# Where the steps of differential attention stand among the projections of a two-layer diffusion trunk

## The chip, the cores and the metric

The kernel runs on one core of a Trainium2 chip. A core has a matrix engine (TensorE, PE in the profile; its weight loads are PEld), a vector engine (VectorE, DVE), an activation engine (ScalarE, ACT), a general engine (GpSimd, POOL), and a queue from which all of this kernel's transfers are issued (SyncE, SP). The engines run side by side and wait for each other by semaphores; within one engine the order of instructions is fixed when the program is built. The metric is the device time of one execution in microseconds. Lower is better. The time before is the median of three runs.

## What is computed

Two layers run over 128 context tokens and 512 latent tokens, 640 columns in all. A layer projects its modulated input into nine parts, runs three mixers on them (a gated convolution, differential attention with 4 heads, latent attention with 8), projects their joined outputs back, and then runs a gated feed-forward block. The part that the change moves is the score and softmax of differential attention for the latent tokens:

```python
def diff_block(qb):
    sc = jnp.einsum("bhmqd,bhmkd->bhmqk", qb, k_all).astype(jnp.float32) * DIFF_SCALE
    p = jax.nn.softmax(sc, axis=-1)
    a = p[:, :, 0] - lam * p[:, :, 1]
    return jnp.einsum("bhqk,bhkd->bhqd", a.astype(v_all.dtype), v_all)
```

Each head has two maps of 32 features; the second, times a learned `lam`, is taken off the first. The keys are the 512 latent tokens and 128 cached ones. The latent attention that follows is an ordinary softmax over heads of 96 features, whose queries and keys are projected up from compressed rows (`cq`, `ckv`).

## The kernel before

Activations lie transposed, 128 features by 640 tokens. Token columns are split into region A (384 columns) and region B (256). A weight is split into a high and a low part, and so is an activation, so that one product is three matmuls (`matmul3`, line 338 on, with its matmul at L343). One `job` (L346) takes one 128-column block of a weight over both regions: with 8 blocks of features it is 24 matmuls for A and 24 for B.

The input projections run in the order `ax0 ac0 ab0 ax1 dk0 dq0 dk1 dq1 dv ckv0 ckv1 ac1 ab1 cq0 cq1 cq2` (`stage_in`, L1036). `dk` and `dq` are the keys and queries of differential attention, two head pairs each. After `dq0` and `dq1` the split rows are written to memory (`ddq`, `ddk`) and read back as 96-row tiles `dqp`, `dkp` that stack the three products (`assemble_diff`, L933; all through the sync queue, L273). `dv` (`dv_job`, L978, matmuls at L992) goes by token tiles, in the order 2, 0, 1, 3, 4, with 24 matmuls each. Then `attention` (L1449) runs up-projections: `k0` to `k3` (keys), `v0` to `v5` (values), `e0`, `e1` (rotary part of the queries) and `q0` to `q3` (queries), in the order of `JOBS` (L77). `q_job` (L1152) evacuates its result on ScalarE (L1160), splits it and writes it to memory (`qd`). `load_pair` (L1172) reads the queries and keys of two latent heads back as `mq` and `mk` (8 loads, and one more of `pd` for the context tokens).

Among these jobs, the kernel places attention work in numbered steps. `plan_steps` (L1380) makes a list: 32 differential steps (0 to 31: four units of 8 scores), then 32 latent ones. A differential step (`score` in `diff_unit`, L1215) is one score of 128 queries against 640 keys: two matmuls (L1192) into the PSUM buffer `sc`, the row maximum on VectorE (L1196), the exponential on ScalarE (L1207), the reciprocal (L1224), and the scaling on GpSimd (L1226) or, for the second map, the combination on VectorE (L1230). Other work is tied to step numbers: the products with the values (five parts for each unit; transposes at L1267, matmuls at L1278) lie four steps and more after their unit, `ASM` (L79) says after which steps the second head pair of `dqp` and `dkp` is assembled, and `LOADS` (L62) after which steps a latent pair is loaded.

`STEPS` (L72) and `JSTEPS` (L78) say how many steps each job runs. A pair is (in the middle, between regions A and B; at the end). The entries of `dv` count steps after each token tile, by the tile's number. From `dq1` on PSUM has two buffers for jobs and the single buffer `sc` for scores (`mm`, L239).

```python
ps = self.job(lambda k, p: u[:, p, 128 * k:128 * k + 128], h, NK, "AB", mid)
self.in_evac(l, n, ps, "AB")
...
self.step(end)
```

These places are the order in which the program is written down. When it is built, a planner sets each engine's queue: it follows the written order as a priority, with its own model of when each instruction would be ready, so that an instruction that it thinks not ready yet can be passed by later ones. The queue that comes out is fixed.

Of the kernel before, what the change touches and what calls it, by code (L numbers as in the profile page):

```python
# [58 lines left out]
ADV = 0  # L59
ACV = 2  # L60
HOLD = 2
LOADS = (29, 37, 43, 52)  # L62
SIDE = ((34, 37), (37, 40, 43), (36, 40), (47, 50, 56), (44, 47), (49, 51), (51, 54), (60, 62))
ADA_N = 12
ADA_IN = 1
# [3 lines left out]
ADA_FF2 = 1  # L69
ADA_LAG = 3  # L70
LAG = 4
STEPS = {"dv": (1, 2, 1, 1, 1), "ckv0": (0, 1), "ckv1": (0, 2), "ac1": (0, 2), "ab1": (0, 2), "cq0": (0, 2), "cq1": (0, 1), "dk1": (0, 0), "dq1": (0, 0)}  # L72
PAT = "PPPt"
PATC = "Pc"
CKS = 30
NP = 6
JOBS = "k0 k1 k2 k3 v0 v1 v2 v3 v4 e0 v5 e1 q0 q1 q2 q3".split()  # L77
JSTEPS = ((0, 1), (0, 1), (0, 1), (3, 0), (0, 1), (1, 0), (0, 0), (0, 0), (0, 1), (0, 2), (0, 0), (0, 0), (0, 1), (0, 0), (2, 1), (1, 0))  # L78
ASM = (9, 15)  # L79


WIN = (("ax0", 0), ("ac0", 512), ("ab0", 256), ("ax1", 128), ("dk0", 1024), ("dq0", 768), ("dk1", 1152),
# [110 lines left out]
class Trunk:  # L193
# [784 lines left out]
    def dv_job(self, l):  # L978
# [8 lines left out]
        for j in (2, 0, 1, 3, 4):  # L987
# [18 lines left out]
            self.tick()  # L1006
            self.step(STEPS["dv"][j])

# [27 lines left out]
    def stage_in(self, l):  # L1036
# [41 lines left out]
        for n in names[nskew:]:  # L1078
# [4 lines left out]
            else:  # L1083
                u = self.W.get((n, l))
                mid, end = STEPS.get(n, (0, 0))
                ps = self.job(lambda k, p: u[:, p, 128 * k:128 * k + 128], h, NK, "AB", mid)
# [293 lines left out]
    def plan_steps(self, l):  # L1380
# [7 lines left out]
        def put(step, *fs):  # L1388
            self.after.setdefault(step, []).extend(fs)
# [11 lines left out]
        def unit(kind, p, hf, n):  # L1401
            hold = {}
            g0 = len(self.steps)

            def start():
                hold["u"] = kind(l, p, hf)

            def step(i):
                if i == 0:
                    start()  # L1410
                hold["u"][0][i]()

            def av(kt):
                if kt == 0:
                    _, tiles, v, dst = hold["u"]
                    hold["av"] = self.av_steps(tiles, v, dst, hf)
                hold["av"][kt]()
            for i in range(n):
                self.steps.append(lambda i=i: step(i))
            for kt in range(5):  # L1420
                put(g0 + n - 1 + LAG + (n * kt) // 5, lambda kt=kt: av(kt))

        for kind, p, hf in units:
            unit(kind, p, hf, 8 if kind == self.diff_unit else 4)
        for g, i in enumerate(ASM):
            put(i, lambda g=g: self.assemble_diff(1, 2 * g, 2 * g + 2))
        for p, i in enumerate(LOADS):
            put(i, lambda p=p: self.load_pair(p))
# [20 lines left out]
    def attention(self, l):  # L1449
# [7 lines left out]
        kinds = {"k": self.k_job, "v": self.v_job, "e": self.qpe_job, "q": self.q_job}  # L1457
        for (kind, j), n in zip(JOBS, JSTEPS):
            n = n if isinstance(n, tuple) else (0, n)
# [251 lines left out]
```

## Time and profile before

| | before |
|---|---|
| median of 3 runs | 1777.19 us (1774.91 to 1778.72) |
| profiled execution | 1775.88 us |
| its span | 1774.1 us |
| TensorE busy | 1702.8 us |
| VectorE busy | 1021.1 us |
| ScalarE busy | 590.6 us |
| GpSimd busy | 420.0 us |

Times in the views are microseconds from the start of the span, of one profiled execution. In a timeline a line gives start, length, engine, line of code, operation, output and inputs, shape and count; in brackets stands how long the engine was idle before it and what released it. A group of matmuls of one kind is merged into one line. Matmuls overlap, so the last of a group ends somewhat into the next.

### The profile page before, as it was taken

What the parts mean: (1) busy time and instruction counts of PE and PEld (TensorE: products, weight loads), DVE (VectorE), ACT (ScalarE), POOL (GpSimd) and SP (SyncE); (2) the same over time, 40 slices, a digit from 0 to 9 for tenths busy, and PEclk for the clock granted to TensorE, in tenths of its full rate; (3) what the DMA queues carried; (4) which work ended last, traced back from release to release, by engine and by line L of the source; (5) the groups of instructions that cost most, each with busy time, mean ns of one, the idle gap of its engine ahead of it and who ended that gap; (6) DMA issues with size and microseconds to landing.
All of it is one profiled execution on the core that took longest, in us unless ns stands there. A gap on an engine that the chain in (4) does not pass through costs nothing. (4 is left out here: it accounts for less than half of the span.)

```text
span 1774.1 us, 29684 instructions
## 1 busy us (share of the span) xinstructions
PE 1702.8 (96%) x11983; PEld 1593.7 (90%) x11983; DVE 1021.1 (58%) x1824; ACT 590.6 (33%) x1010; POOL 420.0 (24%) x400
## 2 busy tenths in 40 slices
PE   8999989998999999999999899899989999999997
PEld 6998867698999999999989798677989999999997
DVE  3656776759566566856397558764682332232236
ACT  1334545525321121122243436554442212211221
POOL 0011113447701010110377111233582000000014
PEclk9999989999999999999989899899999999999998
DMA  9564584321355444544314544722122222222211
GB/s 333 196 204 140 168 250 145 109 90 48 101 149 150 149 136 140 174 130 150 93 51 166 170 113 149 210 64 84 48 75 81 72 75 81 64 79 84 68 53 59
DMA packets 100872, 217.38 MB, mean 123 GB/s; under 512 B 12160, under 2 KB 28928, under 8 KB 100736
## 3 DMA queue, kind: packets, MB, share of 16 engines
q1 hardware_dynamic: 100736, 215.50, 39.3%
q8 instruction: 94, 1.54, 0.4%
q14 instruction: 42, 0.34, 0.1%
HBM read 185.28 MB, written 30.18 MB: 121 GB/s over the span
## 5 line engine op out<-in xcount | busy, mean ns | idle before, releaser
L343 PE MATMUL mm<-h,wu 128*128 128x384 f32 (+1 forms) x4944 | 735.9, 310 | 0.2
L343 PEld LDWEIGHTS mm<-h,wu 128*128 128x128 f32 x4944 | 724.9, 189 | 6.9 <-issue 5.3
L142 ACT CAST wu<-stg 128x1024 fp32r<-128x1024 f32 (+2 forms) x200 | 201.5, 1011 | 701.3 <-issue 347.1
L144 DVE TENSOR_TENSOR wu<-stg,wu 128x1024 fp32r<-128x1024 f32 (+2 forms) x200 | 246.0, 1234 | 145.6 <-ACT wu L142 143.9
L343 PE MATMUL mm<-gh,wu 128*128 128x256 f32 (+1 forms) x1184 | 258.8, 310 | 0.0
L343 PEld LDWEIGHTS mm<-gh,wu 128*128 128x128 f32 x1184 | 198.7, 188 | 0.9 <-issue 0.6
L343 PE MATMUL mm<-gl,wu 128*128 128x384 f32 (+1 forms) x592 | 182.8, 309 | 0.0
L1196 DVE TENSOR_REDUCE nm<-mm 128x1 f32<-128x640 f32 x128 | 104.7, 818 | 54.7 <-PE mm L1192 53.8
L1545 DVE TENSOR_TENSOR gs<-gs,mm 128x640 f32<-128x640 f32 (+2 forms) x48 | 36.6, 763 | 152.7 <-PE mm L343 147.6
L653 DVE SCALAR_TENSOR_TENSOR x<-mm,ga,x 128x512 f32<-128x512 f32 x48 | 35.9, 749 | 146.2 <-PE mm L343 146.2
L672 POOL TENSOR_TENSOR accS<-x 128x640 f32<-128x640 f32 x4 | 10.0, 2490 | 443.6 <-DVE x L659 418.5
L343 PEld LDWEIGHTS mm<-gl,wu 128*128 128x128 f32 x592 | 111.4, 188 | 0.2 <-issue 0.2
L512 DVE SCALAR_TENSOR_TENSOR acc<-rawt,scT,acc 128x512 f32<-128x512 f32 x98 | 75.8, 773 | 57.8 <-DMA rawt<-in_w_ada 56.1
L364 PE MATMUL mm<-h,wu 128*128 128x384 f32 (+1 forms) x576 | 95.6, 329 | 1.0 <-DVE v L694 0.5
L364 PEld LDWEIGHTS mm<-h,wu 128*128 128x128 f32 x576 | 91.5, 206 | 3.3 <-issue 0.8
L343 PE MATMUL mm<-hi,wu 128*128 128x384 f32 (+1 forms) x400 | 89.8, 311 | 0.1
L510 POOL TENSOR_SCALAR acc<-rawt,scT 128x512 f32<-128x512 f32 x14 | 9.8, 701 | 313.0 <-PE tr L527 312.9
L1192 PE MATMUL mm<-mk,mq 96*128 96x384 f32 (+1 forms) x384 | 75.3, 337 | 5.8 <-ACT P L1207 2.3
L517 DVE SCALAR_TENSOR_TENSOR rawt<-rawt,scT 128x512 f32<-128x512 f32 x98 | 74.7, 763 | 2.1 <-POOL rawt L510 2.1
L1192 PEld LDWEIGHTS mm<-mk,mq 96*128 96x128 f32 x384 | 64.1, 201 | 12.7 <-ACT P L1207 4.9
L343 PEld LDWEIGHTS mm<-hi,wu 128*128 128x128 f32 x400 | 68.0, 188 | 2.6 <-issue 1.5
L1207 ACT ACTIVATE P<-mm,nm 128x640 f32<-128x640 f32 x56 | 44.6, 797 | 57.3 <-DVE nm L1196 45.0
(279 smaller groups left out, 2446.8 us busy)
## 6 DMA issues: line engine op xcount, KB each, us to landing
stg<-in_w_ff SPq DMA_DIRECT2D x104, 512.0 KB, 3.6
rawt<-in_w_ada SPq DMA_DIRECT2D x160, 256.0 KB, 3.0
stg<-in_w_in SPq DMA_DIRECT2D x30, 512.0 KB, 4.4
stg<-in_w_ff SPq DMA_DIRECT2D x32, 448.0 KB, 3.3
raw<-in_w_ada SPq DMA_DIRECT2D x32, 256.0 KB, 6.2
stg<-in_w_out SPq DMA_DIRECT2D x16, 512.0 KB, 4.3
mk<-kd SPq DMA_DIRECT2D x32, 240.0 KB, 5.8
mq<-qd SPq DMA_DIRECT2D x32, 192.0 KB, 5.5
```

Of the source, the lines that this page charges most:

```text
L142: nc.scalar.copy(u[:, 0, :ncol], t[:, :ncol])
L144: (nc.gpsimd if self.lo_pool else nc.vector).tensor_sub(u[:, 1, :ncol], t[:, :ncol], u[:, 0, :ncol].bitcast(F32))
L343: self.last = nc.tensor.matmul(out, w(k, pw), x(k, px), start=(k == 0 and i == 0), stop=(k == nk - 1 and i == 2)).ins
L364: self.last = nc.tensor.matmul(ps[:, c0:c1], u[:, pw, 128 * k:128 * k + 128], x(k, px)[:, c0:c1], start=(k == 0 and i == 0), stop=(k == nk ...
L512: nc.vector.scalar_tensor_tensor(self.acc[0], w, c[0], self.acc[0], ALU.mult, ALU.add)
L517: nc.vector.scalar_tensor_tensor(self.acc[1], w, c[1], self.acc[1], ALU.mult, ALU.add)
L653: nc.vector.scalar_tensor_tensor(lat(x), lat(ps), ga[:, 0, s, m:m + 1], lat(x), ALU.mult, ALU.add)
L672: nc.gpsimd.tensor_add(self.accS[:, c0:c1], self.first[0][:, c0:c1], x[:, c0:c1])
L1192: nc.tensor.matmul(ps[:, 128 + c0:128 + c1], q[:96, qc:qc + 128], k[:96, c0:c1], start=(i == 0), stop=(i == len(pairs) - 1))
L1196: nc.vector.tensor_reduce(nm, s, axis=AX.X, op=ALU.max, negate=True)
L1207: self.exp_end = nc.scalar.activation(P, s, AF.Exp, bias=nm, accum_out=sm).ins
L1545: nc.vector.tensor_mul(gs[:, c0:c1], gs[:, c0:c1], ps[:, c0:c1])
```

## The change

Constants only. The steps stand at other jobs; `ASM` and `LOADS` move by some steps.

```diff
-LOADS = (29, 37, 43, 52)
+LOADS = (28, 36, 43, 52)
...
-STEPS = {"dv": (1, 2, 1, 1, 1), "ckv0": (0, 1), "ckv1": (0, 2), "ac1": (0, 2), "ab1": (0, 2), "cq0": (0, 2), "cq1": (0, 1), "dk1": (0, 0), "dq1": (0, 0)}
+STEPS = {"dv": (1, 1, 0, 1, 1), "ckv0": (1, 1), "ckv1": (1, 1), "ac1": (1, 1), "ab1": (1, 1), "cq0": (1, 1),
+         "cq1": (1, 1), "cq2": (1, 1)}
...
-JSTEPS = ((0, 1), (0, 1), (0, 1), (3, 0), (0, 1), (1, 0), (0, 0), (0, 0), (0, 1), (0, 2), (0, 0), (0, 0), (0, 1), (0, 0), (2, 1), (1, 0))
-ASM = (9, 15)
+JSTEPS = ((0, 1), (0, 1), (0, 1), (0, 1), (0, 0), (0, 1), (0, 0), (0, 1), (0, 0), (0, 1), (0, 0), (0, 1), (1, 1), (1, 1),
+          (1, 1), (0, 0))
+ASM = (8, 12)
```

Counted out, so many of the 32 differential steps are written down by the end of each job:

| job | before | after |
|---|---|---|
| `dv`, after tiles 2, 0, 1, 3, 4 | 1, 2, 4, 5, 6 | 0, 1, 2, 3, 4 |
| `ckv0`, `ckv1`, `ac1`, `ab1` | 7, 9, 11, 13 | 6, 8, 10, 12 |
| `cq0`, `cq1`, `cq2` | 15, 16, 16 | 14, 16, 18 |
| `k0`, `k1`, `k2`, `k3` | 17, 18, 19, 22 | 19, 20, 21, 22 |
| `v0`, `v1`, `v2`, `v3`, `v4` | 23, 24, 24, 24, 25 | 22, 23, 23, 24, 24 |
| `e0`, `v5`, `e1` | 27, 27, 27 | 25, 25, 26 |
| `q0`, `q1`, `q2`, `q3` | 28, 28, 31, 32 | 28, 30, 32, 32 |

Before, most jobs of the input projections run two steps at their end; after, one in the middle and one at the end. The parts of the products with the values keep their step numbers and move with them. The second half of the `dqp`, `dkp` tiles is asked for after steps 8 and 12 instead of 9 and 15, the first latent pair after step 28 (middle of `q1`) instead of 29 (middle of `q2`), the second after 36 instead of 37. Both layers use the same constants. Instructions are neither added nor taken away.

## Rows read from the trace of the kernel before

**Rows 1.** The page: busy tenths and granted clock of TensorE, 40 slices

```profile
PE 1702.8 (96%) x11983; PEld 1593.7 (90%) x11983; DVE 1021.1 (58%) x1824; ACT 590.6 (33%) x1010; POOL 420.0 (24%) x400
PEclk9999989999999999999989899899999999999998
```

**Rows 2.** Windows, first layer: length, then busy by engine (instructions), clock, DMA share, GB/s

```profile
100.00:185.00 85.00, 83.33 (x630) 77.81 (x629) 51.55 (x107) 36.04 (x70) 13.55 (x15) 1.00 0.52 158
185.00:240.00 55.00, 53.27 (x366) 43.61 (x364) 44.53 (x90) 35.11 (x67) 7.10 (x7) 1.00 0.57 183
```

**Rows 3.** Timeline of TensorE, second layer, before and at the first score

```profile
959.82 11.91 PE L343 MATMUL mm<-h,wu 128*128 128x384 f32 x83
971.56 3.35 PE L992 MATMUL mm<-wu,h 128*128 128x288 f32 x24
982.19 0.87 PE L1192 MATMUL mm<-dkp,dqp 96*128 96x384 f32 x2 [7.28 <-DMA dkp<-ddk]
```

**Rows 4.** Timeline of the sync queue: first load of dkp, second layer

```profile
978.43 0.59 SPq L273 DMA_DIRECT2D dkp<-ddk  x1
```

**Rows 5.** Windows at low clock: length, TensorE busy (matmuls), clock, DMA share, GB/s

```profile
978.10:985.30 7.20, 3.11 (x13) 0.54 0.85 245
1016.30:1019.70 3.40, 3.40 (x13) 0.50 0.76 173
244.90:258.50 13.60, 11.04 (x47) 0.50 1.04 306
1118.80:1129.00 10.20, 7.63 (x26) 0.50 1.01 326
```

**Rows 6.** Timeline of TensorE, first layer: the first score

```profile
103.19 0.46 PE L1192 MATMUL mm<-dkp,dqp 96*128 96x384 f32 x2
```

**Rows 7.** Timeline of TensorE, first layer: last dv tile, fourth score

```profile
114.68 3.46 PE L992 MATMUL mm<-wu,h 128*128 128x288 f32 x24
...
119.55 0.45 PE L1192 MATMUL mm<-dkp,dqp 96*128 96x384 f32 x2
```

**Rows 8.** Timeline of TensorE: scores that waited, first and second layer

```profile
136.41 0.56 PE L1192 MATMUL mm<-dkp,dqp 96*128 96x384 f32 x2 [1.57 <-ACT Pt L1207]
...
1015.36 0.55 PE L1192 MATMUL mm<-dkp,dqp 96*128 96x384 f32 x2 [1.53 <-ACT Pt L1207]
```

**Rows 9.** Timeline of ScalarE, second layer, around the same place

```profile
1011.41 0.80 ACT L1207 ACTIVATE Pt<-mm,nm 128x640 f32<-128x640 f32 x1 [4.22 <-DVE nm L1196]
...
1012.19 0.68 ACT L892 COPY raw<-mm 128x640 f32<-128x640 f32 x1
```

**Rows 10.** Timeline of TensorE: last differential and first latent scores, both layers

```profile
243.05 0.56 PE L1192 MATMUL mm<-dkp,dqp 96*128 96x384 f32 x2 [1.89 <-ACT P L1207]
246.08 0.90 PE L1192 MATMUL mm<-dkp,dqp 96*128 96x384 f32 x2 [2.47 <-ACT P L1207]
...
249.29 1.65 PE L1192 MATMUL mm<-mk,mq 96*128 96x384 f32 x5 [0.40 <-DMA mk<-kd]
...
1117.54 0.56 PE L1192 MATMUL mm<-dkp,dqp 96*128 96x384 f32 x2 [1.89 <-ACT P L1207]
1119.94 0.90 PE L1192 MATMUL mm<-dkp,dqp 96*128 96x384 f32 x2 [1.83 <-ACT P L1207]
...
1124.77 1.65 PE L1192 MATMUL mm<-mk,mq 96*128 96x384 f32 x5 [1.23 <-DMA mk<-kd]
```

**Rows 11.** Timeline of TensorE, first layer: transposes of the probabilities

```profile
198.92 0.66 PE L1267 MATMUL tr<-first,Pt 128*128 128x128 f32 x4 [0.68 <-ACT PT L267]
```

**Rows 12.** Timeline of ScalarE, first layer: an exponential and the evacuation of q0

```profile
230.34 0.80 ACT L1207 ACTIVATE P<-mm,nm 128x640 f32<-128x640 f32 x1
...
231.12 0.70 ACT L1160 ACTIVATE mqs<-mm 128x640 f32<-128x640 f32 x1
```

**Rows 13.** Timeline of the sync queue, first layer: write of q0, first load

```profile
233.76 0.52 SPq L273 DMA_DIRECT2D qd<-lo  x1
...
237.39 0.54 SPq L273 DMA_DIRECT2D mq<-qd  x1
```

## The prediction

> **What bounds the kernel.** I read the page first. TensorE is busy for 1702.8 of 1774.1 us, so 71 us of its queue are idle, and the row of granted clocks falls below full speed in only a few of its forty slices [rows 1]. Anything worth having is therefore in the stretches where TensorE stands still or runs at 1.2 GHz. The windows by stage show where the change works: in the first layer the projections of the inputs (100 to 185 us) and the up-projections (185 to 240), in the second layer the same from 971 on. In the first layer TensorE is the fullest engine there, but VectorE is busy 51.55 of 85 us (61%) in the first stretch and 44.53 of 55 (81%) in the second, so a step that moves from the second to the first moves from a crowded place to a roomier one [rows 2]. Then I read TensorE's own queue in order of time, for every idle stretch and its releaser; the stretches that differential scores cause are the terms below. The profiled execution took 1775.88 us (span 1774.1), 1.3 under the median of the three runs, 1777.19. I make the sum against 1775.88 and move it by 1.3 at the end.
>
> **Part 1: the first score, one dv tile later.** In the second layer TensorE ends the first tile of `dv` (24 matmuls, 3.35 us) at 974.9 and then stands for 7.28 us before the first score, released by the load of `dkp` [rows 3]. That load is issued at 978.43 [rows 4]; its data come from `dq0`, through memory and back, so nothing of this path depends on how many dv matmuls have run. After the change one more tile of 24 matmuls stands ahead of the score. Its weights are those of the first tile, which has just run with them, so I take its time as the first one's, 3.35 us, and the wait left is 7.28 - 3.35 = 3.9 us. The clock: in 978.1 to 985.3 it averaged 0.54 with 3.11 us of work in it [rows 5]; work at half speed takes double, so this costs 3.11/2 = 1.6 us. The wait of 3.9 is longer than the 1.53 us that lowered the clock elsewhere (part 2), so I count no gain there. Value 3.35. Ends: 0, if the second tile can't start for want of a PSUM buffer until the score does; 7.28 + 1.6 = 8.9, if the planner sets the score later still. The value lies where the named work lies. In the first layer the same score started without a wait at 103.19 [rows 6], so moving it is worth nothing there; its cover is that TensorE has dv tiles to run instead.
>
> **Part 2: one score per half job instead of two at a job's end.** Before, six scores are due within `dv`, and then two at the end of each of four jobs. They can't keep that pace: in the first layer the last dv tile starts at 114.68, and the fourth score comes only at 119.55, in the next job [rows 7]. So scores queue up and meet. TensorE then waits 1.57 us at 136.41 and 1.53 us at 1015.36 for the exponential of the score ahead (only one PSUM buffer, `sc`, is for scores) [rows 8]. In the second layer the reason is to be seen in ScalarE's queue: it waits 4.22 us for a score's maximum, and the copy of `ckv0` that would free the other PSUM buffer stands behind that, at 1012.19 [rows 9]. There the clock fell too: 1016.3 to 1019.7 at 0.50 with 3.40 us of work, a cost of 1.7 us [rows 5]. After the change, 4 scores are due by the end of dv, then one per half job. Half a job is 24 matmuls; 83 take 11.91 us [rows 3], so 24 take 3.4 us. Successive scores that wait only for each other start 3.03 us apart in the first layer (243.05, 246.08) and 2.40 in the second [rows 10]. 3.4 is more than either, so a score's buffer is free when the next is due, and the pairs don't form. Value 1.57 + 1.53 + 1.7 = 4.8 us. Ends: 4.8, and below nothing: the planner times the whole list anew, and waits of the same kind (1.5 each, with a clock stretch 3.2) can form elsewhere: -3.2.
>
> On the clock, the row shows 1.53 us of idle time followed by half speed [rows 5, 8]. The Trainium skill ("TensorE: Matmul & The Clock Gate", Part 1: The HAM clock gate) says that the default is the low clock and that it returns after a whole idle window; by its figures such a short gap would not have lowered it, and the sum would lack the 1.7 us. The trace disagrees with that here, and the measurement decides.
>
> **Part 3: products with the values.** The five parts of each unit follow step numbers, which stay; two of them sat in `k3` with three scores and now lie one to a job. The wait of 0.68 us at 198.92, for the copy between transposes [rows 11], should go. Value 0.7, ends 0 and 0.7.
>
> **Part 4: the end of the differential scores.** Before, 16 steps are left from `k0` on, after 14: two scores leave the stretch where VectorE is at 81%. In before the last scores run with nothing beside them: 1.89 and 2.47 us of waits in the first layer, 1.89 and 1.83 in the second [rows 10], and the clock is at 0.50 in 244.9 to 258.5 with 11.04 us of work and in 1118.8 to 1129 with 7.63 [rows 5], costing 5.5 and 3.8. It looks as if 8.1 + 9.3 us could be had. But the loads for the first latent-attention heads end there as well: right after the last differential score TensorE waits for `mk`, 0.40 at 249.29 and 1.23 at 1124.77 [rows 10]. Their chain starts at `q0`: ScalarE evacuates it at 231.12 [rows 12], the write of its second half is issued at 233.76, the first load that reads it at 237.39 [rows 13], and the second score waits for it until 249.29. The change moves the request for this pair (9 DMAs) one step and one job up, past the writes of `q1`; but it still must follow the write of `q0` by those 3.6 us, and behind it on the sync queue now stand the writes of `q1`, whose readers, the second pair's loads, come seven steps later. Nothing in the plan makes the evacuation of `q0` earlier. So the exposed scores go and the wait for `mk` takes their place: value 0. Ends: the gain 8.1 + 9.3 = 17.4, and a loss, rival 3.
>
> **Part 5: the rest.** `assemble_diff` comes one and three steps earlier (4 DMAs each); its tiles are first read at steps 16 and 18, so it is hidden by at least four steps of 2.4 us. The later pairs' loads move by one step of the latent attention. No instruction is added or removed. Value 0.
>
> **Sum.** 3.35 + 4.8 + 0.7 + 0 = 8.9. I take off 0.7 for a wait between new neighbours, estimated as one of the size of that at 198.92 [rows 11], since the planner sets all orders anew. Gain 8.2: 1775.9 - 8.2 = 1767.7 on the profiled execution's scale, 1769.0 on the median's.
>
> **Rivals.** Rival 1: the end of the scores opens as well, if `q0`'s writes come earlier because VectorE has two scores less behind it. For it: the 81%. Against it: the evacuation at 231.12 is in ScalarE's order, not VectorE's. Half of the 17.4 on top: 1777.2 - 8.2 - 8.7 = 1760.3.
> Rival 2: only part 1 holds, the pairs meet at other places: 1777.2 - 3.4 = 1773.8. For it: scores ran later than their steps in before [rows 7], so steps are only wishes to the planner.
> Rival 3, slower: `q0`'s evacuation gets later. The change puts scores in the middle and at the end of `q0`, `q1` and `q2`, and an exponential that stands ahead of the evacuation in ScalarE's queue holds it, and with it the chain to `mk`, by a score's period. In before one stood directly ahead, at 230.34 [rows 12]. If two more do in each layer, `mk` lands 6.1 and 4.8 us later (twice 3.03 and 2.40), TensorE waits that long, and the gain of 8.2 turns into a loss of 2.7; with a longer half-clock stretch as in part 2 (1.7 each) it is 6.1: 1783.3. It decides from two exponentials on; one costs 2.4 to 3.0 a layer and the change stays level or faster. Against it: the new plan asks for 26 scores before `q0`, the old one for 27.
> Rival 4: it doesn't do what it says, the planner's order hardly moves, or gains and new waits cancel: 1777.
>
> **Chances.** What a measurement of this kernel can tell from no change is about 0.2%, 3.6 us. Forecast (1765 to 1773) 0.42; rival 1 0.12; rival 2 0.20, which lies on the bound, half faster and half the same; rival 4 0.10; rival 3 0.16. Faster 0.42 + 0.12 + 0.10 = 0.64, same 0.20, slower 0.16. The range reaches into half of rival 1 and into the milder half of rival 3: 1760 to 1781. The forecast's own range is 1765 to 1773.
>
> **What would show it.** Part 1: in the second layer 48 dv matmuls ahead of the first score and a wait of about 3.9 us for `dkp`. Part 2: no wait for an exponential of over 1 us before the projections end, and full clock from 990 to 1060. Part 4: at the end of `q3` waits named `mk`, not the exponential. I am wrong if the first score still follows 24 matmuls, if the wait for `mk` grows past 3 us, or if waits for exponentials move into `cq0` to `k1`.

## The result: slower by about 12 us

| | before | after |
|---|---|---|
| runs, us | 1774.91, 1776.75, 1777.19, 1778.72 | 1787.01, 1787.68, 1791.06 |
| profiled execution and its span | 1775.88, 1774.1 | 1787.68, 1785.6 |
| time over before | 1 | 1.0068 (1.0053 to 1.0083) |

The forecast was 1769.0, range 1760 to 1781, with 0.64 on faster. The kernel went the other way. A fourth run of the changed kernel took 2086.61 us at a mean granted clock of 0.745 (0.975 to 0.979 in the other three) and is not compared. The lines of the changed kernel are two further down: L345 is what was L343, L1194 what was L1192, L1209 what was L1207. Its page, TensorE's row and the granted clock, beside [rows 1]:

```profile
PE 1707.8 (96%) x11983; PEld 1598.8 (90%) x11983; DVE 1021.7 (57%) x1824; ACT 591.6 (33%) x1010; POOL 417.1 (23%) x400
PEclk9999979999999999999989899899999999999998
```

As many instructions as before and 5 us more of TensorE's time, with a lower clock in the sixth slice, where the first layer's scores end. The other 6.5 us are idle.

**Where it went.** I cut both layers at the first matmul of a job and take differences of the start times in TensorE's timeline, us:

| kernel | first layer: `dv` to `k0` | `k0` to `v0` | `v0` to `q2` | `q2` to first latent score | latent attention | second layer: `dv` to `k0` | `k0` to `v0` | `v0` to `q2` | `q2` to first latent score | latent attention |
|---|---|---|---|---|---|---|---|---|---|---|
| before | 84.67 | 20.78 | 26.43 | 14.90 | 108.28 | 90.57 | 19.18 | 25.43 | 13.89 | 101.30 |
| after | 84.95 | 23.20 | 24.64 | 21.29 | 107.92 | 90.75 | 22.93 | 24.57 | 16.79 | 99.64 |

The sums are 505.43 and 516.69: 11.3 of the 11.5 us of span. The head of both layers, where most of the steps were moved and where the forecast looked for its gain, is level. The loss stands in two places: from `q2` to the first latent score (the tail), 6.4 us in the first layer and 2.9 in the second, and from `k0` to `v0`, 2.4 and 3.75; of these 15.5 us the stretches behind them give 4.7 back (`v0` to `q2` 1.79 and 0.86, latent attention 0.36 and 1.66). A single row of such a table is no better than its profile: with the same order in the first layer, its latent attention took 108.28 in the kernel before and 105.98 in that of experiment 11. The same places in windows (length, then busy time of each engine with instructions, clock, DMA share, GB/s), second layer `k0` to `v0` and the tail, first layer's tail; before:

```profile
1062.10:1081.30 19.20, 18.88 (x121) 15.20 (x120) 16.64 (x38) 14.09 (x29) 1.60 (x2) 1.00 0.62 213
1106.70:1120.60 13.90, 9.91 (x60) 8.00 (x59) 11.27 (x22) 9.68 (x19) 1.68 (x3) 0.93 0.84 260
231.90:246.80 14.90, 10.54 (x89) 8.55 (x90) 11.23 (x23) 9.39 (x17) 2.09 (x3) 0.93 0.93 265
```

and after:

```profile
1068.20:1091.10 22.90, 19.69 (x122) 15.03 (x121) 19.31 (x41) 14.26 (x30) 1.68 (x3) 1.00 0.51 162
1115.70:1132.50 16.80, 11.36 (x60) 9.44 (x59) 12.23 (x23) 9.98 (x19) 1.60 (x2) 0.85 0.88 279
231.90:253.20 21.30, 14.74 (x109) 11.55 (x108) 12.15 (x26) 9.90 (x19) 1.72 (x3) 0.76 0.90 275
```

The second pair of lines is the plainest: the same 60 matmuls, 2.9 us longer, half of it idle time and half the lower clock (0.85 against 0.93). TensorE's timeline of the changed kernel at the steps of the forecast, the second layer's first `dv` tile, first score and eighth score, with [rows 3, 8] as their counterpart:

```profile
977.47 3.35 PE L994 MATMUL mm<-wu,h 128*128 128x288 f32 x24
987.18 0.87 PE L1194 MATMUL mm<-dkp,dqp 96*128 96x384 f32 x2 [6.37 <-DMA dkp<-ddk]
...
1021.14 0.56 PE L1194 MATMUL mm<-dkp,dqp 96*128 96x384 f32 x2 [2.42 <-ACT Pt L1209]
```

The first score still follows 24 `dv` matmuls, although it is now written behind the second tile, and what its wait lost (0.91) the eighth score's gained (0.89). Now the two places of the loss, second layer: the 17th and 18th score and the first matmul of `k1`; then the 30th score, the first matmul of `q3` and the 32nd score.

```profile
1070.85 0.56 PE L1194 MATMUL mm<-dkp,dqp 96*128 96x384 f32 x2 [0.37 <-ACT Pt L1209]
...
1073.89 0.56 PE L1194 MATMUL mm<-dkp,dqp 96*128 96x384 f32 x2 [1.89 <-ACT Pt L1209]
1074.47 0.44 PE L345 MATMUL mm<-ckh,wu 128*128 128x384 f32 x1
...
1123.86 0.63 PE L1194 MATMUL mm<-dkp,dqp 96*128 96x384 f32 x2 [2.48 <-ACT P L1209]
1124.46 0.69 PE L345 MATMUL mm<-hi,wu 128*128 128x384 f32 x1
...
1131.82 0.90 PE L1194 MATMUL mm<-dkp,dqp 96*128 96x384 f32 x2 [2.73 <-ACT P L1209]
```

Before, `k1` (1065.18) stood between the 17th and the 18th score (1064.22, 1068.42) and `q3` between the 29th and the 30th:

```profile
1111.86 0.56 PE L1192 MATMUL mm<-dkp,dqp 96*128 96x384 f32 x2
1112.45 0.44 PE L343 MATMUL mm<-hi,wu 128*128 128x384 f32 x1
...
1115.19 0.46 PE L1192 MATMUL mm<-dkp,dqp 96*128 96x384 f32 x2
```

Now no job stands between them, and TensorE waits for an exponential that a job used to cover. Why the jobs are late is in ScalarE's timeline at the same two places:

```profile
1072.95 0.80 ACT L1209 ACTIVATE Pt<-mm,nm 128x640 f32<-128x640 f32 x1 [1.67 <-DVE nm L1198]
...
1073.73 0.68 ACT L894 COPY raw<-mm 128x640 f32<-128x640 f32 x1
...
1122.93 0.79 ACT L1209 ACTIVATE P<-mm,nm 128x640 f32<-128x640 f32 x1 [2.15 <-DVE nm L1198]
...
1123.71 0.69 ACT L1162 ACTIVATE mqs<-mm 128x640 f32<-128x640 f32 x1
```

The second line evacuates `cq2`, the fourth `q1`. Each frees the PSUM buffer that the next job but one writes (jobs have two), and each stands behind an exponential that waits for its score's maximum. They end at 1074.41 and 1124.40; `k1` starts at 1074.47 and `q3` at 1124.46.

The first layer's tail reads otherwise. ScalarE's evacuation of `q1`, then TensorE from the 30th score to `q3`, and a window over `q3`:

```profile
240.01 0.69 ACT L1162 ACTIVATE mqs<-mm 128x640 f32<-128x640 f32 x1
...
240.16 0.90 PE L1194 MATMUL mm<-dkp,dqp 96*128 96x384 f32 x2 [1.59 <-ACT P L1209]
243.58 0.66 PE L436 MATMUL tr<-rawt,scT 128*32 128x128 f32 x8 [2.51 <-DMA rawt<-in_w_ada]
244.58 0.65 PE L436 MATMUL tr<-rawt,scT 128*32 128x128 f32 x8 [0.35 <-DMA rawt<-in_w_ada]
245.16 0.69 PE L345 MATMUL mm<-hi,wu 128*128 128x384 f32 x1
...
245.10:250.20 5.10, 5.10 (x24) 5.04 (x20) 2.61 (x6) 0.00 (x0) 0.00 (x0) 0.50 1.06 302
```

`q3`'s PSUM buffer is free at 240.70, but transposes of two modulation weights (`rawt`) stand ahead of it and wait 2.86 us for their loads, and `q3` then runs at a granted clock of 0.50. Before, these 16 transposes stood behind the first latent score. The exponentials are waited for less than before (1.59 and 2.02 us against 1.89 and 2.47). On the sync queue the first of these weights' loads (238.52) stands behind two of the first pair's loads (237.67, 238.04).

The second layer gave the theory: *an exponential ahead of an evacuation in ScalarE's queue keeps a job from covering the next score.* The rivals: A, the loads and assemblies that are asked for earlier cost the time as traffic; B, the even spread of the head does; and, later, any new order costs as much. In the first layer's tail the rows are nearer to A.

### The profile page after: what moved, and what is told of

Read it like the earlier page. It is cut to its first block, busy times and chain, and to the rows that moved or that the text cites. A ratio compares the mean times of both kernels' runs of the same rounds, so it can differ in the third digit from the quotient of the medians.

```text
span 1785.6 us, 29690 instructions
## 1 busy us (share of the span) xinstructions
PE 1707.8 (96%) x11983; PEld 1598.8 (90%) x11983; DVE 1021.7 (57%) x1824; ACT 591.6 (33%) x1010; POOL 417.1 (23%) x400
## 5 line engine op out<-in xcount | busy, mean ns | idle before, releaser
L345 PE MATMUL mm<-h,wu 128*128 128x384 f32 (+1 forms) x4944 | 735.4, 310 | 0.4
L345 PEld LDWEIGHTS mm<-h,wu 128*128 128x128 f32 x4944 | 724.7, 189 | 6.4 <-issue 4.3
L345 PE MATMUL mm<-gh,wu 128*128 128x256 f32 (+1 forms) x1184 | 258.9, 310 | 0.0
L345 PEld LDWEIGHTS mm<-gh,wu 128*128 128x128 f32 x1184 | 198.9, 188 | 0.9 <-issue 0.6
L345 PE MATMUL mm<-gl,wu 128*128 128x384 f32 (+1 forms) x592 | 183.0, 310 | 0.0
L345 PEld LDWEIGHTS mm<-gl,wu 128*128 128x128 f32 x592 | 111.3, 188 | 0.2 <-issue 0.2
L345 PE MATMUL mm<-hi,wu 128*128 128x384 f32 (+1 forms) x400 | 93.0, 320 | 0.0
L1194 PE MATMUL mm<-mk,mq 96*128 96x384 f32 (+1 forms) x384 | 73.5, 334 | 4.8 <-ACT P L1209 3.3
L1194 PEld LDWEIGHTS mm<-mk,mq 96*128 96x128 f32 x384 | 63.6, 200 | 11.0 <-ACT P L1209 6.9
L345 PEld LDWEIGHTS mm<-hi,wu 128*128 128x128 f32 x400 | 70.5, 195 | 3.0 <-issue 1.9
L345 PE MATMUL mm<-lo,wu 128*128 128x384 f32 (+1 forms) x200 | 63.3, 317 | 0.0
```

The costliest lines, as they stand in the source:

```text
L345: self.last = nc.tensor.matmul(out, w(k, pw), x(k, px), start=(k == 0 and i == 0), stop=(k == nk - 1 and i == 2)).ins
L1194: nc.tensor.matmul(ps[:, 128 + c0:128 + c1], q[:96, qc:qc + 128], k[:96, c0:c1], start=(i == 0), stop=(i == len(pairs) - 1))
```

## The experiments

All ratios are to the kernel before, run beside each version; its median was 1775.3 to 1776.3 there. "Built order" is the order of the instructions on a queue in the program as built, which the trace then shows. Where an edit adds lines to the kernel, the same instructions carry other line numbers (the score's matmuls are L1196 in experiment 8, for example).

**1. Middle steps to the jobs' ends.** In the changed kernel:

```
"cq2": (1, 1) -> (0, 2);  JSTEPS of q0, q1, q2: (1, 1) -> (0, 2)
```

> The changed kernel, but in the jobs cq2, q0, q1 and q2 the score step that was put in the middle is put at the end, two there; requests of loads and assemblies stay as changed. In the built order of ScalarE's queue the evacuation of cq2 now stands ahead of the next exponential and that of q1 ahead of the next one too; on TensorE k1 again follows one score behind k0, and q3 stands one score earlier than in the changed kernel. Theory (an exponential that stands ahead of an evacuation keeps a PSUM buffer from the next job but one): the 3.4 us at k1 and the 2.7 to 3 us at q3 of each layer go, the loss of about 12 us is gone, 1775 to 1780. Rival A (the loads and assemblies that are asked for earlier cost it): nothing comes back, 1785 to 1791. Rival B (the even spread over the first projections costs it): nothing comes back either.

1786.54, ratio 1.0061 (1.0049 to 1.0073): nothing came back. The expectation was wrong because it looked at `k1` alone. `k1` does follow one score again, but now the exponential of the 18th score is ahead of `k0`'s evacuation, so `k2` is late: `k0` to `v0` takes 23.31 in the second layer (after 22.93). The tail there is repaired (13.76), the stretch `v0` to `q2` is worse (27.02). A blocked evacuation was handed on, not removed.

**2. Requests as before.** In the changed kernel:

```
LOADS = (28, 36, 43, 52) -> (29, 37, 43, 52);  ASM = (8, 12) -> (9, 15)
```

> The changed kernel with the requests of the latent-attention loads and of the assembled keys as before (29, 37, 43, 52 and 9, 15); all score steps as changed. In the built order the exponential still stands ahead of cq2's evacuation in both layers and k1 behind the second score, but q1's evacuation is ahead of the exponential again, and q3 stands one score earlier than in the changed kernel. Theory: the k1 loss stays (about 3.4 us a layer), the q3 loss goes (about 3 a layer): 1780 to 1784. Rival A (the moved requests cost it as traffic): all comes back, 1777. If both halves cost the same whatever the order: 1787.

1781.85, ratio 1.0033 (1.0021 to 1.0045): half comes back. The tails are 15.87 and 13.89, nearly or quite those of before; `k0` to `v0` stays at 22.98 and 22.21. Experiment 5 will give as much back by one of these numbers, so the assemblies and the second pair add nothing that can be told.

**3. The head alone.** In the kernel before, the changed steps in `dv` to `cq1`:

```
STEPS of before -> dv (1, 1, 0, 1, 1) and (1, 1) for ckv0, ckv1, ac1, ab1, cq0, cq1
```

> The kernel before with the changed steps in dv to cq1 alone (16 steps by the end of cq1 in both), the rest and all requests as before. In the second layer both queues are as before from cq2 on; in the first layer one score more is done there by the end of the stretch. Theory: the head costs nothing and gives next to nothing: the first score still follows 24 dv matmuls, starts 0.9 us earlier, and the wait of the eighth score grows by as much; 1774 to 1778. Rival B (the even spread of the head costs the 12 us): 1785 or more. The blind prediction's parts 1 and 2: 1769.

1777.13, ratio 1.0010 (1.0001 to 1.0019). Rival B falls: the spread in the head neither gains nor costs more than the 0.2% that can be told from no change.

**4. Two steps into `cq2`.** In the kernel before:

```
STEPS + "cq2": (1, 1);  JSTEPS of k0, k1: (0, 1), (0, 1) -> (0, 0), (0, 0)
```

> The kernel before with one thing changed: the two steps at the ends of k0 and k1 are asked for in the middle and at the end of cq2, so that in the built order an exponential stands ahead of cq2's evacuation and k1 behind one more score. All requests as before. Theory: k1 starts some 3.4 us later in each layer as in the changed kernel, without any moved load: 1782 to 1786. Rival A (moved requests): 1777. In the first layer q3 is built one score later as well, which by the theory adds up to 3: up to 1787.

1786.95, ratio 1.0067 (1.0054 to 1.0080): without one moved load this edit alone costs as much as the whole change. ScalarE at that place, then TensorE:

```profile
1067.99 0.80 ACT L1207 ACTIVATE Pt<-mm,nm 128x640 f32<-128x640 f32 x1 [1.80 <-DVE nm L1196]
...
1068.77 0.68 ACT L892 COPY raw<-mm 128x640 f32<-128x640 f32 x1
```

```profile
1068.93 0.56 PE L1192 MATMUL mm<-dkp,dqp 96*128 96x384 f32 x2 [1.60 <-ACT Pt L1207]
...
1070.31 0.84 PE L343 MATMUL mm<-ckh,wu 128*128 128x384 f32 x2
```

The exponential, `cq2`'s copy behind it, the wait that `k1` should have covered, and then `k1` at half clock (0.84 for two matmuls, where a pair takes 0.52 in the kernel before; the granted clock is 0.50 from 1070.2 to 1072.0). But only part of the time stands here: in the second layer `k0` to `v0` grew by 0.6 and `v0` to `q2` by 4.2, with parts of the products with the values next to each other, waiting 0.44 and 1.05 us for their copies, and `q2` 0.72 for the evacuation of `q0`. That all of this is the same mechanism is not shown. Experiment 2 has the same two steps in `cq2` and costs half as much, so the price of this place depends on where the later steps stand.

**5. The first pair's loads one step later.** In the changed kernel:

```
LOADS = (28, 36, 43, 52) -> (29, 36, 43, 52)
```

> The changed kernel with one number changed: the loads of the first latent-attention pair are asked for at step 29, as before the change, not 28 (in the changed kernel step 28 is the one in the middle of q1). By the built order the first 27 scores are as in the changed kernel but for one; then q1's evacuation, which in the changed kernel waits on a transfer's semaphore and stands behind the next exponential, has no such wait and stands ahead of it, and q3's matmuls stand one score earlier. Theory (the pair's 8 tiles, taken ahead of q1's own output tile, make that one wait for a buffer, so q1's PSUM buffer comes free a score later and q3 no longer covers a score): the loss between q2 and the first latent-attention score goes, about 2.9 us in the second layer and 3 to 6 in the first: 1778 to 1782. Rival (any new order of the stretch from k0 on costs as much; the place of the evacuation has nothing to do with it): 1785 to 1790.

1780.15, ratio 1.0029 (1.0019 to 1.0039): seven of the twelve us for one number. The tails fall to 15.78 and 13.89, `k0` to `v0` gives nothing back (23.18 and 24.86). ScalarE in the second layer, two exponentials with `q1`'s evacuation between them:

```profile
1118.14 0.80 ACT L1207 ACTIVATE Pt<-mm,nm 128x640 f32<-128x640 f32 x1
...
1118.92 0.70 ACT L1160 ACTIVATE mqs<-mm 128x640 f32<-128x640 f32 x1
...
1121.18 0.80 ACT L1207 ACTIVATE P<-mm,nm 128x640 f32<-128x640 f32 x1 [0.90 <-DVE nm L1196]
```

The program as built says why a load reaches into ScalarE's order. In the changed kernel `q1`'s output tile lies in the buffer of a `hi` half of `e1` that a write to memory still reads, and its evacuation carries a wait for that transfer; here, and before the change, it lies in a buffer that has long been free, and carries none. `load_pair` at step 28 comes in the middle of `q1` and takes eight tiles of the same pool of 31 first. On the chip the buffer was not what was late: in the changed kernel the evacuation starts 0.78 us behind the start of the exponential ahead of it (1122.93, 1123.71), without a wait. The order that the planner had made of it was. In the first layer the modulation weights' loads (239.58) now stand ahead of the pair's first load (241.67), and no transpose waits for them.

**6. Exponentials held behind the evacuations.** In the changed kernel, steps and requests as changed; a score's matmuls and maximum stay, its exponential and what follows are written later:

```
job cq2, q0, q1, q2: step(mid) keeps exp() back; flush() behind the job's evacuation
cq2's last step: exp() kept back until behind k0's evacuation
```

> The changed kernel, all steps and requests in their changed places; only the exponentials of the scores asked for in cq2, q0, q1 and q2 are written later in the program: that of a middle step behind the evacuation of its job, that of cq2's last step behind the evacuation of k0. Scores' matmuls and maxima stay where they are. In the built order cq2's and k0's evacuations stand ahead of the exponentials again and k1, k2, k3 follow one score each, as before the change; the tail stays as in the changed kernel (q3 behind one more score). Theory: the 3 to 4 us lost between k0 and v0 in the second layer and the 1 to 3 of the first come back, the tail's loss stays: 1781 to 1784. Rival: 1785 to 1790.

1782.27, ratio 1.0036 (1.0023 to 1.0048). ScalarE in the second layer:

```profile
1065.40 0.79 ACT L1226 ACTIVATE Pt<-mm,nm 128x640 f32<-128x640 f32 x1 [2.17 <-DVE nm L1213]
...
1066.65 0.70 ACT L903 COPY raw<-mm 128x640 f32<-128x640 f32 x1
...
1068.43 0.80 ACT L1226 ACTIVATE Pt<-mm,nm 128x640 f32<-128x640 f32 x1 [0.31 <-DVE nm L1213]
```

`cq2`'s copy is ahead of the next exponential again, and the 1.89 us wait of the 18th score is gone. From `k0` to `v0` 1.35 of the 3.75 us come back (21.58). The rest stays, in waits of at most 0.62 us. The transposes of the probabilities and their products stand about one score earlier there than in the kernel before; whether that is the rest was not tried. The second layer's tail stays at 16.28, as the theory says for it. The first layer's falls from 21.29 to 18.87, which it had not said, so not all that comes back is the price of `cq2`'s evacuation.

**7. Both repairs.**

```
experiment 6 with LOADS of experiment 5
```

> Both at once: the changed kernel with the pair's loads at step 29 and the held exponentials. From k0 on the second layer's built order is close to that of the kernel before, with all steps where the change put them. Theory: nearly all of the loss is gone, 1773 to 1779. Rival: 1785 to 1790. If the two causes overlap (one alone already gives all back): as the better one of the two alone.

1781.67, ratio 1.0033 (1.0021 to 1.0046): no better than either alone, which the theory did not expect. The second layer does what it says: `k0` to `v0` 21.57, tail 13.88, in all 2.6 us behind the kernel before instead of 4.3. In the first layer the tail is 20.68, and TensorE's timeline shows a wait in it:

```profile
251.74 0.66 PE L445 MATMUL tr<-rawt,scT 128*32 128x128 f32 x8 [4.08 <-DMA rawt<-in_w_ada]
```

Transposes of a modulation weight, put at every second step from 32 (`ada`), stand ahead of the first latent score there, since one more score is done by then; before, they stood behind it, where they waited 0.99. In the changed kernel the waits for them were the 2.51 and 0.35 ahead of `q3`.

**8. The first score really behind the second tile.** In the kernel before, second layer alone:

```
the first score's matmuls issue after the last matmul of dv's second tile; dv (1, 2, 1, 1, 1) -> (2, 2, 0, 1, 1)
```

> The kernel before, with the first score of the second layer alone tied behind the last matmul of the second dv tile, as the words of the change say; every later step as before. In the built order 48 dv matmuls stand ahead of it and scores 6 and 7 have only transposes between 7 and 8. The blind prediction's part 1: the wait for the loaded keys falls from 7.28 to about 3.9 us, 3.35 less: 1772 on these runs. Rival (the scores behind it come no later, they meet again and the time is given back in waits for the exponentials of scores 6 and 7): the wait falls by as much and the time stays at 1775.

1776.64, ratio 0.9995 (0.9986 to 1.0004). TensorE, the second `dv` tile and the first, seventh and eighth score of the second layer, then a window behind the eighth:

```profile
976.03 3.48 PE L993 MATMUL mm<-wu,h 128*128 128x288 f32 x24 [0.48 <-ACT dq L919]
983.00 0.87 PE L1196 MATMUL mm<-dkp,dqp 96*128 96x384 f32 x2 [3.49 <-DMA dkp<-ddk]
...
1012.00 0.56 PE L1196 MATMUL mm<-dkp,dqp 96*128 96x384 f32 x2 [1.90 <-ACT Pt L1211]
1014.39 0.90 PE L1196 MATMUL mm<-dkp,dqp 96*128 96x384 f32 x2 [0.90 <-ACT Pt L1211]
...
1013.60:1020.40 6.80, 6.00 (x19) 5.93 (x20) 4.17 (x8) 3.76 (x8) 0.80 (x1) 0.50 0.56 128
```

The wait falls by 3.8, where part 1 had worked out 3.4. Of this, 0.5 is a new wait ahead of the second tile, for the copy of `dq1` out of PSUM; 1.3 is back at the seventh and eighth score (2.80 in place of 1.53); and behind the eighth the clock is at 0.50 with 6.00 us of work in it, in the kernel before with 3.40 [rows 5], which at half speed is 1.3 more. At `k0` the layer is 0.6 ahead, at the first latent score still 0.6.

**9. All modulation parts one step later**, on experiment 7:

```
put(32 + 2 * i, ...) -> put(33 + 2 * i, ...)
```

> The kernel of the run with both repairs (pair's loads at step 29, exponentials held behind the evacuations), and the twelve modulation parts put at every second step from 33, not from 32. Why: in that run's first layer TensorE waited 4.08 us for a modulation weight (rawt) in front of the first latent-attention score, since four of its transposes stood ahead of that score in the built order, which they don't in the kernel before. With 33 they don't again; the order is otherwise the same. Theory (a third cost of its own, from the first layer having one score more behind it there): 3 to 4 us come back, 1777 to 1779. Rival (something else is awaited at that place anyway, the loads of the first pair or the last exponential): no change, 1780 to 1783.

1782.90, ratio 1.0047 (1.0034 to 1.0059). The first layer's tail falls by the 4.6 us (16.12), and the latent attention behind it takes 6.0 longer (111.08 against 105.06), 2.1 of it idle time and the rest busy time at a mean clock of 0.94 against 0.98. A wait was removed where it stood; what eleven other parts did was not foreseen.

**10 and 11. Parts 1 and 2 as they were meant**, the kernel before with the first score tied as in 8 and

```
dv (2, 1, 0, 1, 1), ckv0 (0, 1), ckv1 (0, 1), ac1 (0, 2), ab1 (0, 3), cq0 (0, 2), cq1 (0, 2)
```

in both layers (10) or the second alone (11).

> The kernel before, with the first score of the second layer tied behind the second dv tile and, in dv to cq1 of both layers, other numbers of steps (in the order of writing: dv tiles 0, 2, 1, 1, 1; ckv0 1, ckv1 1, ac1 2, ab1 3, cq0 2, cq1 2), the same 16 by the end of cq1. In the built order of both layers 32 matmuls stand between scores 7 and 8, and from k0 on the second layer is as before. This is the blind prediction's parts 1 and 2 as they were meant. If they were sized rightly once the order does what the change's words say: 3.35 from the first wait, 1.57 and 1.53 from the waits at score 8, 1.7 from the clock, about 8: 1767 to 1769. Rival (scores are the chain: what is not waited for here is waited for later): 1774 to 1776. In the first layer the order from cq1 on differs as well, which may cost up to 2.

> The same in the second layer alone; the first layer is built exactly as in the kernel before. If parts 1 and 2 are sized rightly: 3.35 + 1.53 + 1.7 = 6.6 less, 1768 to 1771. Rival (given back later in the stretch): 1774 to 1776.

1775.67, ratio 0.9997 (0.9987 to 1.0006), and 1774.68, ratio 0.9993 (0.9984 to 1.0003): no change that can be told. In the profile of 11 the second layer is 5.6 us ahead at `k0` (85.01 against 90.57), near the 6.6 that parts 1 and 2 promised; `k0` to `v0` then gives 2.5 back. A part of the lead is luck: the load that the first score waits for landed 0.7 us sooner than in the kernel before. In the two profiles 2.6 and 3.1 us of the lead are still there at `v0`; the intervals of all runs reach down to 2.3 and 2.8 us less.

**12. The pair's loads earlier in the kernel before.**

```
LOADS = (29, 37, 43, 52) -> (27, 37, 43, 52)
```

> The kernel before with one number changed: the first pair's loads are asked for at step 27 (q0's end), not 29 (the middle of q2). Up to score 28 both layers are built as before; then the pair's 8 tiles are taken ahead of q1's own output tile, which gets a buffer that a transfer still reads, its evacuation stands behind the exponential of score 29, and q3's matmuls behind score 30 in both layers, as in the changed kernel. Theory: the tail's loss shows in the kernel before, 2.9 us in the second layer and 3 to 6 in the first: 1781 to 1784. Rival (it needs the changed steps as well): 1775 to 1777.

1779.67, ratio 1.0024 (1.0014 to 1.0034): slower by 4, from one number, with every step where it was. ScalarE and TensorE in the second layer:

```profile
1117.40 0.79 ACT L1207 ACTIVATE P<-mm,nm 128x640 f32<-128x640 f32 x1 [2.15 <-DVE nm L1196]
1118.18 0.69 ACT L1160 ACTIVATE mqs<-mm 128x640 f32<-128x640 f32 x1
```

```profile
1118.34 0.56 PE L1192 MATMUL mm<-dkp,dqp 96*128 96x384 f32 x2 [2.46 <-ACT P L1207]
1118.93 0.48 PE L343 MATMUL mm<-hi,wu 128*128 128x384 f32 x1
...
1126.41 0.90 PE L1192 MATMUL mm<-dkp,dqp 96*128 96x384 f32 x2 [2.74 <-ACT P L1207]
```

These are the rows of the changed kernel over again: `q1`'s evacuation behind the exponential with its 2.15, `q3` behind the 30th score with its 2.46 (2.48), 2.74 at the last (2.73). The tails are 18.27 and 16.91, 3.4 and 3.0 more than before. With experiment 5 this shows from both sides that the early request costs the tails. In the first layer the way is again another one: no score waits there from the 30th on, and TensorE waits for a modulation weight, whose load (241.74) stands behind all eight of the pair (238.04 to 241.27):

```profile
248.70 1.35 PE L434 MATMUL tr<-rawt,scT 128*32 128x128 f32 x16 [5.66 <-DMA rawt<-in_w_ada]
```

No run separates the two ways. The price in all runs, 4, is under the 6.4 of the two tails and under the expectation; the latent attention behind them took 2.1 less in this profile.

**13. The spread with the same order from `k0` on.** As 11, with `ab1` (1, 2), `cq0` (1, 2), `cq1` (0, 1).

> As the spread in the second layer alone, but with the sixteen steps placed so that score 16 comes ahead of k0 and one score after it (ab1 1 in the middle and 2 at the end, cq0 the same, cq1 1 at the end); from k0 on both queues of the second layer are built exactly as in the kernel before. In the run before this one the second layer was 5.6 us ahead at k0 and gave 2.5 back by v0, where score 17 came 1.9 us later behind k0 than in the kernel before. Theory (the lead is lost only where scores stand closer together than their own chain of matmul, maximum and exponential allows): nothing is given back, the second layer ends 5 us ahead: 1770 to 1772. Rival (the scores' chain sets the pace whatever the places): 2.5 or more given back again, 1774 to 1776.

1775.67, ratio 0.9993 (0.9984 to 1.0002). The waits of the first score, then in `ac1` and at `cq1`, second layer:

```profile
982.80 0.87 PE L1197 MATMUL mm<-dkp,dqp 96*128 96x384 f32 x2 [4.07 <-DMA dkp<-ddk]
...
1024.08 0.73 PE L815 MATMUL mm<-first,ny 128*128 128x128 f32 x5 [1.38 <-DVE ny L337]
1041.00 1.50 PE L345 MATMUL mm<-h,wu 128*128 128x384 f32 x7 [1.14 <-DVE y L890]
```

3.2 us less at the first score, 1.53 less at the eighth (1.23 in its place at the seventh), and 2.5 in new waits for VectorE. In the 8.6 us behind the first score the clock averages 0.64, in the kernel before 0.81. At `k0` the layer is 0.2 ahead, and from `k0` to `v0` it gives 0.3 back. The time is the rival's, its reason is not: the lead was lost ahead of `k0`, to the clock and to waits for VectorE's normalisations, and not to the scores' chain behind it.

**14. One modulation part one step later**, on experiment 7:

```
put(32 + 2 * i, ...) -> put(max(33, 32 + 2 * i), ...)
```

> The run with both repairs, and only the first of the twelve modulation parts moved from step 32 to 33; the other eleven stay. In the run in which all twelve moved, the first layer's stretch from q2 to the first latent score fell from 20.7 to 16.1 us, but the latent attention behind it took 6 us longer. Theory (the wait of 4.08 us for a modulation weight in front of the first latent score is a cost of its own, and the 6 us were the price of moving the other parts): the stretch stays at 16 to 17 us and the attention behind it at 105, in all 1777 to 1779. Rival (the time lost at the end of the scores only moves into the attention): 1780 to 1783.

1781.63, ratio 1.0036 (1.0023 to 1.0049), the tail 20.84 with the wait at 3.93: the part moved behind one more score and still stands ahead of the first latent one. The expectation had not looked that far in the order, and the question stays as experiment 9 left it.

No version beat the kernel before by more than the measurement can tell.

## Why the prediction was wrong

**Part 1, 3.35 us.** The forecast's lower end came true: 0. The step that failed first is that the score would move with its number: it still followed 24 matmuls, and 0.9 was gained and given back. The reason was not the one named for that end, a missing PSUM buffer: the step's number is only where the score is written, and the planner put it where it stood before. Forced behind the tile (8) the wait fell as worked out, by 3.8 against 3.35, and the time did not. The second step that failed is that a wait of TensorE is worth its length; of 3.8, 0.5 came back as a wait ahead of the second tile (for a PSUM buffer, the reason named for the lower end, but small), 1.3 at the seventh and eighth score, and 1.3 in the clock behind them.

**Part 2, 4.8 us.** "The pairs don't form" was wrong. The scores of [rows 8] still meet, and wait 1.83 and 2.42 in place of 1.57 and 1.53. Between `k0` and `k1` a new wait of 1.89 came, which the last sentence of the prediction named as a sign that it is wrong. The argument had compared half a job's 3.4 us with a score's 2.4 to 3.0, as if the steps were kept; rival 2 had said that steps are only wishes, though it kept part 1. But where the spread was really made (10, 11, 13), it moved waits about and earned nothing that can be told. In 10, 11 and 13 the wait of 1.53 and the 1.7 us of clock behind it were gone, and other waits stood in their place.

**Part 3, 0.7.** Wrong in sign and small: the wait of [rows 11] is gone, and in the first layer four of 0.26 to 0.59, all for VectorE, stand between `k0` and `v0`.

**Part 4, value 0.** Here most of the loss is. Its end on the other side, rival 3 (0.16), named a mechanism that the second layer shows: an exponential ahead of an evacuation in ScalarE's queue. It named the wrong victim. I followed `q0`'s evacuation to the load of `mk`; in the changed kernel TensorE doesn't wait for `mk` at all there (0.40 and 1.23 before). The victim is the PSUM buffer: in the second layer `q1`'s evacuation holds `q3`, and `cq2`'s holds `k1`. Part 2 had read just this for the copy of `ckv0` [rows 9], and the forecast did not ask where the new order would make it again. In the first layer's tail it named nothing that came: modulation weights were no term of the sum. The rival's price, 6.1 us, was about half of what came.

**Parts 4 and 5, the moved requests, value 0.** For the assemblies and the later pairs the nothing was right (2 against 5). For the first pair, in part 4, it is the failing step with the largest price: the request was costed by when its data land. A request also takes its tiles and its place on the sync queue; asking one step earlier cost 7 us (5), and two steps earlier 4 in the other kernel (12).

**What is shown and what is open.** Shown: that the pair's early request costs the tails, by 5 and 12, and row by row how it does so in the second layer; that the head is level, by 3; that `cq2`'s evacuation behind an exponential costs part of `k0` to `v0`, by 6 (1.35 of 3.75 in the second layer), with the same rows in 4. Not shown: the other 2.4 us there, the 2.4 of the first layer in the same stretch (experiment 6 gives 0.9 of them back), and how much of the first layer's tail, the largest single loss, is the modulation weights' wait. Both repairs together give back half of the 12.

## What to carry to other kernels

Where a planner or a queue sets the order, cost a moved step by what it will stand ahead of on each engine, and look first for evacuations: in a kernel with two PSUM buffers for its jobs, an exponential in front of a job's copy takes the cover away from the next score but one. A request that is asked for earlier also takes its buffers and its place on the transfer queue earlier, so list who draws from the same pool, and whose loads stand on that queue, between the old place and the new. And a wait of a full engine is not worth its length until a run has shown that nothing behind it grows.

## What the runs showed of the hardware

The forecast took 1.7 us of low clock after a wait of 1.53 as a cost of the wait. The runs show that such a wait decides nothing by itself. In the kernel before, the wait of 1.57 [rows 8] lies in a stretch whose clock is 1.00 [rows 2]. In nine kernels TensorE's order in the first layer is the same up to `ab1`, with a wait of 1.83 us at the eighth score. In three of them (1, 3 and 5) the clock fell behind it and `ac1` took 11.8 to 12.1 us, in the other six it stayed and `ac1` took 10.5. Windows of 3 us from about 1 us behind the score (136.51 in experiment 3, 135.32 in experiment 6), experiment 3:

```profile
137.50:140.50 3.00, 3.00 (x14) 3.00 (x13) 2.86 (x6) 1.92 (x5) 0.14 (x1) 0.63 0.66 172
140.50:143.50 3.00, 3.00 (x19) 3.00 (x17) 0.14 (x1) 0.00 (x0) 0.00 (x0) 0.80 0.96 200
```

and experiment 6:

```profile
136.30:139.30 3.00, 3.00 (x19) 3.00 (x18) 2.86 (x6) 1.92 (x5) 0.14 (x1) 1.00 0.71 173
139.30:142.30 3.00, 3.00 (x25) 3.00 (x24) 1.14 (x5) 0.00 (x0) 0.00 (x0) 1.00 0.95 199
```

In the first window of each the other engines' work is the same to the hundredth. By the Trainium skill's rule in "TensorE: Matmul & The Clock Gate" (Part 1: The HAM clock gate), on which the forecast weighed this, so short a gap leaves the clock alone: the second pair of rows agrees, the first doesn't.
